# Where weights and moving operands begin in SBUF: offsets modulo 512 bytes

## The chip, the cores and the metric

The kernel runs on one core of a Trainium2 chip as one launch. The metric is the device time of that launch in microseconds. Three runs of the kernel before took 1084.68, 1085.39 and 1087.12 us (median 1085.39); the profiled execution, from which all rows come, took 1085.86 us, of which 1084.1 us are the span from its first to its last instruction.

## The reference

A sequence of 256 tokens of width 1024 goes through three blocks, all in float32. Each block is a mixer followed by a squared-ReLU MLP of width 4096; the three mixers differ. The dense products carry most of the arithmetic:

```python
for l in range(DEPTH):                       # block 1
    h = _rmsnorm(x, ln_mix_g[l])
    proj = h @ w_in[l]                       # 1024 x 7748: attention, HGRN, convolution, gates
    ...
    mixed = (g[:, :, 0] * (y_attn @ w_up_attn[l]) + g[:, :, 1] * (y_hgrn @ w_up_hgrn[l])
             + g[:, :, 2] * (y_conv @ w_up_conv[l]))
    x = x + mixed @ w_out[l]
    h = _rmsnorm(x, ln_mlp_g[l])
    x = x + jnp.square(jax.nn.relu(h @ w_mlp_up[l])) @ w_mlp_down[l]
...
def even_mixer(h, w_in, b_forget, rel_bias, w_out):            # block 2
    qa, ka, va, fa, qb, kb, vb = _split(h @ w_in, SPLIT_AB)
    ...
    return o @ w_out
def odd_mixer(h, positions, w_in, q_norm, kv_norm, w_uq, w_ukv, w_out):   # block 3
    qc, kc, vc, c_q, c_kv, k_r = _split(h @ w_in, SPLIT_CD)
    ...
    return o @ w_out
def squared_relu_mlp(h, w_up, w_down):                         # blocks 2 and 3
    return jnp.square(jax.nn.relu(h @ w_up)) @ w_down
```

## The kernel before

Activations lie transposed: 128 partitions by 8 blocks of 256 tokens. All weights of the program are one stream of 128x128 blocks in the order of their use. SyncE loads the stream in pieces of 2048 columns into `stg` (three buffers). `take` (L163) splits each 1024 columns, 8 blocks, into two parts that TensorE multiplies in one pass each: ScalarE writes the high part `whi` (L173), VectorE the rest `wlo` (L175), five buffers each. Activations are split in the same way: `operand` (L304) writes the high part `xh` and the rest `xl` of the normalized input of a mixer or an MLP, `oh`, `ol` hold the heads' outputs of mixers 2 and 3, `mh`, `ml` the mixed branches of mixer 1, and `hid` the MLP's hidden layer, high part and rest side by side in 512 columns.

A product of one weight block and one activation block is three matmuls of 256 columns (`gemm`, L230, L233, L234): whi with the high part, whi with the rest, wlo with the high part. Each has its own load of 128x128 weights ahead of it. `gemm_wide` (L242, L243) makes the same three products in two matmuls, since `hid` holds both parts side by side: whi with 512 columns, then wlo with the first 256. It is used for seven of the eight output blocks of each down projection; the eighth uses `gemm`. `gemm_tokens` (L269) exchanges the sides: slices of `xh` and `xl` are the loaded weights, and 256 columns of whi or wlo stream.

The order of the work around is set by the program's text and by a scheduler that works from a model of the engines' times: `slot` hands pieces of attention to the engines between output blocks of the dense products, and each engine then has one fixed queue. Weight pieces, ScalarE's and VectorE's splits and attention's softmax run beside TensorE.

Where tiles lie: the pools are laid out one behind another. Small tiles in the pool `keep` (`eps`, `half`, `rtok`, of 4 or 8 bytes, 32 bytes of room each) stand ahead of the weights' pools, so that stg, whi and wlo begin 32 bytes past a multiple of 512. A weight block is 512 bytes in a partition and a block of 256 activations is 1024, so that within a stage every moving operand begins at one and the same distance, modulo 512, from the weights. In the kernel before this distance (moving operand less weights) is 416 bytes for xh and xl in all six stages, 288 for mh and ml, and 0 for hid, oh, ol, the branches' operands and the latents of mixer 3.

In mixer 3 a rotated key is made in the tile `kr` (L1069 to L1076) and two rotated queries in `zr` (two buffers, L1081 to L1086); each is done with `rope` on VectorE and GpSimd.

Of the kernel before, what the change touches and what calls it, by code (L numbers as in the profile page):

```python
# [10 lines left out]
FP32 = mybir.dt.float32  # L11
FP32R = mybir.dt.float32r
# [6 lines left out]
T = 256  # L19
D = 1024  # L20
FF = 4096
KD = 8
# [16 lines left out]
FIRST = 256  # L39

RA, RB, RC = 1.0, 1.5, 1.5

GROUPS_MIX = [range(0, 8)]
GROUPS_ATT = [range(0, 4), range(4, 6), range(6, 8)]
# [20 lines left out]
def _mid(ap, n):  # L65

    return ap.unsqueeze(1).to_broadcast([ap.shape[0], n, ap.shape[1]])
# [8 lines left out]
def kernel(  # L76
# [18 lines left out]
    def pool(name, bufs=1, space=None, stack=ctx):  # L95
        kw = {"space": space} if space is not None else {}
        return stack.enter_context(tc.tile_pool(name=name, bufs=bufs, **kw))

    keep = pool("keep")
# [10 lines left out]
    xv = keep.tile([128, NVEC + KD * T], FP32, name="xv")  # L110
    vec = xv[:, 0:NVEC]
    x = xv[:, NVEC:].rearrange("p (k t) -> p k t", k=KD)
    xh = keep.tile([128, KD, T], FP32R, name="xh")
    xl = keep.tile([128, KD, T], FP32R, name="xl")
    cst = keep.tile([128, NCONST], FP32, name="cst")
    ones = keep.tile([128, 128], FP32, name="ones")
    sqa = keep.tile([128, T], FP32, name="sqa")
    staged = {}

# [12 lines left out]
    load(1)  # L132
    nc.sync.dma_start(out=cst, in_=consts)
    nc.vector.memset(ones, 1.0)
    eps = keep.tile([128, 1], FP32, name="eps")
    nc.vector.memset(eps, EPS)

    half = keep.tile([128, 2], FP32, name="half")
    nc.gpsimd.memset(half, 0.0)
    for g in range(2):  # L140
        nc.gpsimd.memset(half[64 * g:64 * g + 64, g:g + 1], HD ** -0.5)
# [6 lines left out]
    def v_(name, j=0):  # L148
        o = VOFF[name][0] + j
        return vec[:, o:o + 1]  # L150
# [60 lines left out]
    def slot(steps=1):  # L211
        for d in list(due):
            d[0] -= 1
            if d[0] <= 0:
                due.remove(d)
                d[1]()
        credit[0] = credit[0] + steps if chains else 0
        while credit[0] >= 1:
            credit[0] -= 1
            step()  # L220

    def drain():
        while due or chains:
            slot()
# [22 lines left out]
    def gemm1(kt, ah, al, steps=1):  # L247
        ks = kt if isinstance(kt, range) else range(kt)
        ps = pg_p.tile([128, 2, T], FP32, name="pg")
        gemm(ps[:, 0], ks, ah, al)  # L250
        slot(steps * len(ks) / KD)
        return ps[:, 0]
# [51 lines left out]
    def operand(j, gain):  # L304

        nc.scalar.activation(out=xh[:, j], in_=x[:, j], func=AF.Copy, scale=v_(gain, j))
        nc.vector.scalar_tensor_tensor(out=xl[:, j], in0=x[:, j], scalar=v_(gain, j), in1=xh[:, j],  # L307
                                       op0=ALU.mult, op1=ALU.subtract)
# [16 lines left out]
    def sum_squares():  # L325
        ps = po_p.tile([128, 2, T], FP32, name="po")
        nc.tensor.matmul(out=ps[:, 0], lhsT=ones, rhs=sqa, start=True, stop=False)
        nc.tensor.matmul(out=ps[:, 0], lhsT=ones, rhs=sq_last["s"], start=False, stop=True)
        return ps[:, 0]
# [1 line left out]
    rstd = keep.tile([128, T], FP32, name="rstd")  # L331
    rvar = keep.tile([128, T], FP32, name="rvar")

    rtok = keep.tile([128, 2], FP32, name="rtok")

    def rstd_tokens():

# [8 lines left out]
    def residual(ah, al, groups, gain):  # L346


        for ks in groups[:-1]:
            for j in range(KD):  # L350
                nc.vector.tensor_tensor(out=x[:, j], in0=gemm1(ks, ah, al, RC), in1=x[:, j], op=ALU.add)
        drain()
        for j in range(KD):
            nc.vector.tensor_tensor(out=x[:, j], in0=gemm1(groups[-1], ah, al), in1=x[:, j], op=ALU.add)
            operand(j, gain)
            squares(j)

    def mlp(gain_next):
        def variance():
            u = tmp.tile([128, 512], FP32, name="rs_u", bufs=1)[:, 0:T]  # L360
            nc.vector.tensor_scalar(out=u, in0=sum_squares(), scalar1=1.0 / D, scalar2=EPS, op0=ALU.mult, op1=ALU.add)
            nc.vector.reciprocal(out=rvar, in_=u)

        variance()
        with ExitStack() as st:
            hp = pool("hid", stack=st)
            mp = pool("mlpt", 2, stack=st)
            hid = hp.tile([128, FF // 128, 2, T], FP32R, name="hid")
            for j in range(0, FF // 128, 2):
                ps = gemm2(KD, xh, xl)  # L370
                r = mp.tile([128, 2, T], FP32, name="r")
                s = mp.tile([128, 2, T], FP32, name="s")
                nc.scalar.activation(out=r, in_=ps, func=AF.Relu)
                nc.scalar.activation(out=hid[:, j:j + 2, 0], in_=r, func=AF.Square)
                nc.vector.scalar_tensor_tensor(out=s, in0=ps, scalar=0.0, in1=r, op0=ALU.max, op1=ALU.mult)
                nc.vector.tensor_tensor(out=hid[:, j:j + 2, 1], in0=s, in1=hid[:, j:j + 2, 0], op=ALU.subtract)  # L376
            for j in range(KD):

                wide = j < KD - WN
                if wide:  # L380
                    ps = gemm_wide(FF // 128, hid)
                else:
                    ps = gemm1(FF // 128, hid[:, :, 0], hid[:, :, 1])

                for z in HALVES if gain_next is None and j == KD - 1 else [slice(0, T)]:
                    t = tmp.tile([128, T], FP32, name="dn")[:, z]
                    if wide:
                        nc.scalar.activation(out=t, in_=ps[:, 1], func=AF.Copy)
                        nc.vector.tensor_tensor(out=t, in0=ps[:, 0], in1=t, op=ALU.add)
                    nc.vector.tensor_tensor(out=t, in0=t if wide else ps[:, z], in1=rvar[:, z], op=ALU.mult)  # L390
                    nc.vector.tensor_tensor(out=x[:, j, z], in0=t, in1=x[:, j, z], op=ALU.add)  # L391
                    if z.stop - z.start < T:
                        nc.scalar.activation(out=rstd[:, z], in_=x[:, j, z], func=AF.Square)
                if gain_next is not None:
                    operand(j, gain_next)
                    squares(j)
                else:
                    if j < KD - 1:
                        squares(j)
                    nc.scalar.activation(out=xg[:, j], in_=x[:, j], func=AF.Copy, scale=v_("norm_final", j))  # L400
# [132 lines left out]
    with ExitStack() as st:  # L533
# [9 lines left out]
        att = pool("att1", stack=inner)  # L543
# [250 lines left out]
        for j in range(4):  # L794
# [4 lines left out]
            t = hg.tile([128, T], FP32, name="ut", bufs=2)  # L799
# [8 lines left out]
            t = hg.tile([128, T], FP32, name="ut", bufs=2)  # L808
# [9 lines left out]
        for b, (yh, yl) in enumerate(((yc_h, yc_l), (ya_h, ya_l), (yh_h, yh_l))):  # L818
            if b == 2:
                while "linear" not in events:  # L820
                    slot()
                mhp = pool("mixh", stack=late)
                mh = mhp.tile([128, KD, T], FP32R, name="mh")
                ml = mhp.tile([128, KD, T], FP32R, name="ml")
            gates = {}

            def gate(j):
                ps = gemm2(KD, xh, xl)
                z = mp.tile([128, 2, T], FP32, name="gz", bufs=1)
                gates[j] = g = mp.tile([128, 2, T], FP32, name="gg", bufs=2)  # L830
                nc.vector.tensor_tensor(out=z, in0=ps, in1=_mid(rstd, 2), op=ALU.mult)
                sigmoid(g, z, g)

            gate(0)
            for j in range(0, KD, 2):
                if j + 2 < KD:
                    gate(j + 2)
                ps = gemm2(4, yh, yl)
                mj, g = mixed[:, j:j + 2], gates.pop(j)
                if b == 0:  # L840
                    nc.vector.tensor_tensor(out=mj, in0=ps, in1=g, op=ALU.mult)
                else:
                    nc.vector.tensor_tensor(out=g, in0=ps, in1=g, op=ALU.mult)
                    (nc.vector if b == 2 else nc.gpsimd).tensor_tensor(out=mj, in0=mj, in1=g, op=ALU.add)
                if b == 2:
                    split(mh[:, j:j + 2], ml[:, j:j + 2], mj)
# [35 lines left out]
    with ExitStack() as st:  # L882
        att = pool("att2", stack=st)
        pb["p"] = 4
        oh = att.tile([128, KD, T], FP32R, name="oh")
        ol = att.tile([128, KD, T], FP32R, name="ol")
        cb = att.tile([128, 8, T], FP32, name="cb")
        nc.sync.dma_start(out=cb, in_=chk_bias)

# [85 lines left out]
    first(rsqrt(sum_squares(), T, 1.0 / D, rstd))  # L975
    with ExitStack() as st:
        att = pool("att3", stack=st)
        oh = att.tile([128, KD, T], FP32R, name="oh")
        ol = att.tile([128, KD, T], FP32R, name="ol")

        swap = [(i + ROPE_HALF) % 32 for i in range(32)]

# [85 lines left out]
        values(0)  # L1068
        cqh, cql = latent(3, "q_norm", "cq")  # L1069
        ckh, ckl = latent(2, "kv_norm", "ck")  # L1070
        kr = att.tile([128, T], FP32, name="kr")
        ps = gemm1(KD, xh, xl)
        scaled(kr[0:32], ps[0:32])
        a, b = rope(kr, 32)
# [4 lines left out]
        for j in range(2):  # L1079
            ps = gemm1(3, cqh, cql, RA)  # L1080
            zr = att.tile([128, T], FP32, name="zr", bufs=2)  # L1081
# [242 lines left out]
```

## Time and profile before

| | |
|---|---|
| median of three runs | 1085.39 us |
| profiled execution | 1085.86 us |
| its span | 1084.1 us |
| TensorE matmul busy | 1061.3 us, 98%, 8136 matmuls |
| TensorE weight load busy | 1022.7 us, 94% |
| VectorE busy | 838.4 us, 77% |
| ScalarE busy | 601.7 us, 56% |
| GpSimd busy | 156.2 us, 14% |
| HBM read | 181.57 MB, 168 GB/s over the span |

A matmul's busy time overlaps that of the next, so the 98% say that TensorE nearly always has one in flight and not how fast it goes. How fast is read from the timeline: the time from one matmul's start to the next one's, here called a step.

### The profile page before, as it was taken

Reading aid. Unit: us, or ns where it says so; the run is one execution under the profiler, and the core shown is the slowest. Engines: PE = TensorE matmul, PEld = TensorE weight load, DVE = VectorE, ACT = ScalarE, POOL = GpSimd, SP = SyncE. Lnnn points to the kernel's source line nnn. Section 1 sums busy time; section 2 is a strip of 40 time slices with the busy share of each in tenths; the row PEclk is TensorE's granted clock in tenths of the full one; section 3 lists DMA queues with packets and bytes.
Section 4 is the critical chain, followed back from the end, with each engine's and each line's share of the span. In section 5 each row is a group of like instructions: output and inputs, shape, how many; then the busy total and the mean of one; then the engine's idle time right before and its main releaser. Section 6 shows DMA issues by size and latency. Waiting matters only on the chain.

```text
span 1084.1 us, 20315 instructions
## 1 busy us (share of the span) xinstructions
PE 1061.3 (98%) x8136; PEld 1022.7 (94%) x8136; DVE 838.4 (77%) x1613; ACT 601.7 (56%) x944; POOL 156.2 (14%) x174
## 2 busy tenths in 40 slices
PE   7999999999999999999999999999999999999996
PEld 6999989999999988999999999988999999999886
DVE  7999898977996666678778867667689788666673
ACT  6467456665575544456654555444458755554441
POOL 1045550110400001120003000011121021000110
PEclk9999999999999999999999999999999999999999
DMA  8544433555455545554434555555444235555541
GB/s 299 218 161 141 154 121 117 167 189 195 156 195 195 188 182 185 185 210 146 150 130 143 179 177 190 194 194 174 173 161 164 107 118 185 170 190 194 191 159 39
DMA packets 29008, 183.94 MB, mean 170 GB/s; under 512 B 3057, under 2 KB 6385, under 8 KB 7281
## 3 DMA queue, kind: packets, MB, share of 16 engines
q1 hardware_dynamic: 28768, 182.50, 47.7%
q8 instruction: 64, 1.05, 0.4%
q14 instruction: 32, 0.25, 0.1%
q10 hardware_dynamic: 144, 0.13, 0.0%
HBM read 181.57 MB, written 1.05 MB: 168 GB/s over the span
## 4 chain that ended last, share of the span: by engine, by line
PE 90%; DVE 6%; issue 1%; ACT 1%; DMA 1%; POOL 0%; SPq 0%; DVEq 0%; POOLq 0%
PE pg L233 19%; PE pg L234 19%; PE pg L230 19%; PE pg L242 14%; PE pg L243 7%; PE pg L269 4%; DVE wlo L175 3%; PE sc L435 2%; PE po L472 2%; PE pt L465 1%; PE sc L428 1%; PE po L473 1%; DVE xl L307 1%; DMA stg<-w 1%; ACT whi L173 1%
## 5 line engine op out<-in xcount | busy, mean ns | idle before, releaser
L175 DVE TENSOR_TENSOR wlo<-stg,whi 128x512 fp32r<-128x512 f32 (+1 forms) x676 | 472.7, 740 | 163.9 <-ACT whi L173 160.8
L173 ACT ACTIVATE whi<-stg 128x1024 fp32r<-128x1024 f32 (+1 forms) x340 | 356.3, 1051 | 337.0 <-PE pg L233 191.8
L230 PE MATMUL pg<-xh,whi 128*128 128x256 f32 x1472 | 417.6, 284 | 7.3 <-ACT whi L173 6.9
L233 PE MATMUL pg<-xl,whi 128*128 128x256 f32 x1472 | 416.8, 284 | 0.9 <-DVE xl L307 0.7
L234 PE MATMUL pg<-xh,wlo 128*128 128x256 f32 x1472 | 417.1, 284 | 0.3
L230 PEld LDWEIGHTS pg<-xh,whi 128*128 128x128 f32 x1472 | 278.9, 190 | 8.6 <-ACT whi L173 7.2
L233 PEld LDWEIGHTS pg<-xl,whi 128*128 128x128 f32 x1472 | 279.0, 190 | 2.7 <-DVE xl L307 2.0
L234 PEld LDWEIGHTS pg<-xh,wlo 128*128 128x128 f32 x1472 | 278.9, 190 | 1.6 <-DVE wlo L175 1.0
L242 PE MATMUL pg<-hid,whi 128*128 128x512 f32 x672 | 233.1, 391 | 0.0
L243 PE MATMUL pg<-hid,wlo 128*128 128x256 f32 x672 | 188.2, 280 | 0.0
L242 PEld LDWEIGHTS pg<-hid,whi 128*128 128x128 f32 x672 | 125.7, 187 | 27.4
L243 PEld LDWEIGHTS pg<-hid,wlo 128*128 128x128 f32 x672 | 127.0, 189 | 0.0
L315 POOL TENSOR_TENSOR sqa<-xv 128x256 f32<-128x256 f32 x6 | 4.1, 678 | 471.4 <-DVE xv L391 304.4
L319 POOL TENSOR_TENSOR sq<-xv 128x256 f32<-128x256 f32 x36 | 26.5, 742 | 175.2 <-DVE xv L391 169.6
L455 ACT ACTIVATE p<-p,m 128x128 f32<-128x128 f32 x64 | 28.6, 448 | 17.6 <-DVE m L453 17.3
L320 POOL TENSOR_TENSOR sqa<-sqa,sq 128x256 f32<-128x256 f32 x36 | 36.9, 1024 | 2.3
L233 PE MATMUL pg<-ol,whi 128*128 128x256 f32 x128 | 36.8, 289 | 0.1
L269 PE MATMUL pg<-whi,xl 128*128 128x256 f32 x128 | 36.6, 286 | 0.0
L269 PE MATMUL pg<-whi,xh 128*128 128x256 f32 x128 | 36.4, 284 | 0.0
L234 PE MATMUL pg<-oh,wlo 128*128 128x256 f32 x128 | 36.3, 286 | 0.0
L269 PE MATMUL pg<-wlo,xh 128*128 128x256 f32 x128 | 36.2, 283 | 0.0
L376 DVE TENSOR_TENSOR hid<-s,hid 128x512 fp32r<-128x512 f32 x48 | 33.1, 690 | 4.0
(361 smaller groups left out, 1589.8 us busy)
## 6 DMA issues: line engine op xcount, KB each, us to landing
stg<-w SPq DMA_DIRECT2D x168, 1024.0 KB, 4.8
t<-t_bias SPq DMA_DIRECT2D x8, 128.0 KB, 2.9
cb<-chk_bias SPq DMA_DIRECT2D x1, 1024.0 KB, 4.8
xv<-x_in SPq DMA_DIRECT2D x2, 384.0 KB, 6.3
cst<-consts SPq DMA_DIRECT2D x1, 640.0 KB, 11.2
stg<-w SPq DMA_DIRECT2D x1, 512.0 KB, 8.1
out<-xg SPq DMA_DIRECT2D x2, 256.0 KB, 2.9
stg<-w SPq DMA_DIRECT2D x1, 384.0 KB, 6.8
```

Source lines behind the costliest of these rows:

```text
L173: act = [nc.scalar.activation(out=h[:, z], in_=src[:, z], func=AF.Copy) for z in (pieces if u == 0 else [slice(0, UW)])]
L175: dve = [nc.vector.tensor_tensor(out=l[:, z], in0=src[:, z], in1=h[:, z], op=ALU.subtract) for z in pieces]
L230: m0 = nc.tensor.matmul(out=ps, lhsT=h, rhs=ah[:, k], start=(k == ks[0]), stop=False)
L233: nc.tensor.matmul(out=ps, lhsT=h, rhs=al[:, k], start=False, stop=False)
L234: m1 = nc.tensor.matmul(out=ps, lhsT=l, rhs=ah[:, k], start=False, stop=(k == ks[-1]))
L242: nc.tensor.matmul(out=ps, lhsT=h, rhs=a[:, k], start=(k == 0), stop=False)
L243: nc.tensor.matmul(out=ps[:, 1], lhsT=l, rhs=a[:, k, 0], start=False, stop=(k == kt - 1))
L269: nc.tensor.matmul(out=ps, lhsT=a[:, k, t], rhs=w_, start=(k == 0 and i == 0), stop=(k == kt - 1 and i == 2))
L319: nc.gpsimd.tensor_tensor(out=s, in0=x[:, j], in1=x[:, j], op=ALU.mult)
L320: nc.gpsimd.tensor_tensor(out=sqa, in0=sqa, in1=s, op=ALU.add)
L376: nc.vector.tensor_tensor(out=hid[:, j:j + 2, 1], in0=s, in1=hid[:, j:j + 2, 0], op=ALU.subtract)
L455: nc.scalar.activation(out=p[:, a:b], in_=p[:, a:b], func=AF.Exp, scale=-1.0, bias=m[:, i:i + 1], accum_out=sums[:, i:i + 1])
```

## The change

Small tiles of `keep` are put into one tile `few`, so that stg, whi and wlo begin at a multiple of 512 bytes. The tiles of moving operands get 512 bytes more (`ROOM`), and the operand is put at an offset within: `xh` and `xl` are views of one tile `xo`, placed anew for each of the six stages that `PLACES` names, `hid` by `HIDDEN`, mh and ml by `MIXED`, oh and ol by `HEADS` (all in elements of 4 bytes). To make room, `kr` becomes one of the two `zr` buffers.

Distance of the moving operand from the weights modulo 512 bytes:

| stage | operand | before | after |
|---|---|---|---|
| mixer 1 | xh, xl | 416 | 64 |
| mixer 1, output | mh, ml | 288 | 352 |
| MLP 1, up | xh, xl | 416 | 192 |
| MLP 1, down | hid | 0 | 64 |
| mixer 2 | xh, xl | 416 | 32 |
| mixer 2, output | oh, ol | 0 | 64 |
| MLP 2, up | xh, xl | 416 | 320 |
| MLP 2, down | hid | 0 | 192 |
| mixer 3 | xh, xl | 416 | 16 |
| mixer 3, output | oh, ol | 0 | 448 |
| MLP 3, up | xh, xl | 416 | 448 |
| MLP 3, down | hid | 0 | 32 |
| mixer 1, branches; mixer 3, latents | ya, yh, yc; cq, ck | 0 | 0 |

```diff
+ROOM = 128
+PLACES = {"block1": 32, "ln_mlp_g": 64, "norm_mix0": 24, "norm_mlp0": 96, "norm_mix1": 20, "norm_mlp1": 0}
+HIDDEN = {"norm_mix0": 16, "norm_mix1": 48, None: 8}
+MIXED = 16
+HEADS = [16, 112]
...
-    xh = keep.tile([128, KD, T], FP32R, name="xh")
-    xl = keep.tile([128, KD, T], FP32R, name="xl")
+    xo = keep.tile([128, 2 * KD * T + ROOM], FP32R, name="xo")
+
+    def placed(t, n, at):
+        return t[:, at:at + n * T].rearrange("p (k t) -> p k t", k=n)
+
+    def place(stage):
+        nonlocal xh, xl
+        at = PLACES[stage]
+        xh, xl = placed(xo, KD, at), placed(xo, KD, at + KD * T)
...
+    few = keep.tile([128, 16], FP32, name="few")
...
-    eps = keep.tile([128, 1], FP32, name="eps")
+    eps = few[:, 0:1]
...
-    half = keep.tile([128, 2], FP32, name="half")
+    half = few[:, 1:3]
...
-    rtok = keep.tile([128, 2], FP32, name="rtok")
+    rtok = few[:, 4:6]
...
         drain()
+        place(gain)
         for j in range(KD):
...
-            hid = hp.tile([128, FF // 128, 2, T], FP32R, name="hid")
+            hid = hp.tile([128, FF // 128 * 2 * T + ROOM], FP32R, name="hid")
+            hid = placed(hid, FF // 128 * 2, HIDDEN[gain_next]).rearrange("p (k i) t -> p k i t", i=2)
...
+            if gain_next is not None:
+                place(gain_next)
...
-        oh = att.tile([128, KD, T], FP32R, name="oh")
-        ol = att.tile([128, KD, T], FP32R, name="ol")
+        oh = placed(att.tile([128, KD * T + ROOM], FP32R, name="oh"), KD, HEADS[0])
+        ol = placed(att.tile([128, KD * T + ROOM], FP32R, name="ol"), KD, HEADS[0])
...
-        kr = att.tile([128, T], FP32, name="kr")
+        kr = att.tile([128, T], FP32, name="zr", bufs=2)
```

No instruction is added to the engines' work or taken from it. In mixers 1 and 2, in the MLPs and on SyncE and GpSimd the queues hold the same instructions in the same order; in mixer 3 the scheduler puts 10 instructions of ScalarE, 13 of VectorE and 105 of TensorE at other places, two of which follow.

ScalarE in mixer 3, from the second `zr` copy on: `s` is a softplus of the stick-breaking heads, `ck_h` the high part of a latent, `qm` queries, `pT` transposed probabilities. Before:

```order
544 L1082 ACTIVATE zr<-pg 128x256 x2
545 L173 ACTIVATE whi<-stg 128x1024
546 L1090 ACTIVATE qm<-pg 64x256 x2
547 L467 ACTIVATE pT<-pt 128x384
548 L1090 ACTIVATE qm<-pg 64x256 x2
549 L293 ACTIVATE s<-sc 128x384
550 L278 ACTIVATE ck_h<-ck_raw 128x512
551 L294 ACTIVATE s<-s 128x384
552 L1090 ACTIVATE qm<-pg 64x256 x2
```

The same place of ScalarE's queue now:

```order
544 L1106 ACTIVATE zr<-pg 128x256 x2
545 L193 ACTIVATE whi<-stg 128x1024
546 L1114 ACTIVATE qm<-pg 64x256 x2
547 L491 ACTIVATE pT<-pt 128x384
548 L1114 ACTIVATE qm<-pg 64x256 x2
549 L313 ACTIVATE s<-sc 128x384
550 L314 ACTIVATE s<-s 128x384
551 L298 ACTIVATE ck_h<-ck_raw 128x512
552 L1114 ACTIVATE qm<-pg 64x256 x2
```

The split of `ck_h` now stands behind the second step of the softplus. The second `zr` copy has a new wait: its buffer was `kr`, which VectorE must have copied into `km` (L1076, now L1100).

TensorE in mixer 3, ahead of the second product that has tokens on its output rows: the scores of a latent head (`sc<-km,qm`). Before:

```order
6042 L230 MATMUL pg<-xh,whi 128x256
6043 L233 MATMUL pg<-xl,whi 128x256
6044 L428 MATMUL sc<-km,qm 128x128
6045 L435 MATMUL sc<-km,qm 128x256
6046 L234 MATMUL pg<-xh,wlo 128x256
6047 L269 MATMUL pg<-whi,xh 128x256
6048 L269 MATMUL pg<-whi,xl 128x256
```

The same place of TensorE's queue now:

```order
5935 L254 MATMUL pg<-xo,wlo 128x256
5936 L452 MATMUL sc<-km,qm 128x128
5937 L459 MATMUL sc<-km,qm 128x256
5938 L250 MATMUL pg<-xo,whi 128x256
5939 L253 MATMUL pg<-xo,whi 128x256
5940 L254 MATMUL pg<-xo,wlo 128x256
5941 L289 MATMUL pg<-whi,xo 128x256 x2
```

The scores stand two matmuls of 256 columns earlier against the dense product.

## Rows read from the trace of the kernel before

**Rows 1.** The page's head, its busy times, and the chain that ended last.

```profile
span 1084.1 us, 20315 instructions
...
PE 1061.3 (98%) x8136; PEld 1022.7 (94%) x8136; DVE 838.4 (77%) x1613; ACT 601.7 (56%) x944; POOL 156.2 (14%) x174
...
PE 90%; DVE 6%; issue 1%; ACT 1%; DMA 1%; POOL 0%; SPq 0%; DVEq 0%; POOLq 0%
```

**Rows 2.** The costliest groups of TensorE: shapes, count, then busy us, mean ns.

```profile
L230 PE MATMUL pg<-xh,whi 128*128 128x256 f32 x1472 | 417.6, 284 | 7.3 <-ACT whi L173 6.9
...
L242 PE MATMUL pg<-hid,whi 128*128 128x512 f32 x672 | 233.1, 391 | 0.0
L243 PE MATMUL pg<-hid,wlo 128*128 128x256 f32 x672 | 188.2, 280 | 0.0
...
L269 PE MATMUL pg<-whi,xl 128*128 128x256 f32 x128 | 36.6, 286 | 0.0
...
L234 PE MATMUL pg<-oh,wlo 128*128 128x256 f32 x128 | 36.3, 286 | 0.0
```

**Rows 3.** Timeline, TensorE, up projection of MLP 1: start us, duration us, instruction.

```profile
319.96 0.28 PE L234 MATMUL pg<-xh,wlo 128*128 128x256 f32 x1
...
337.56 0.28 PE L234 MATMUL pg<-xh,wlo 128*128 128x256 f32 x1
```

**Rows 4.** Timeline, TensorE, up projection of MLP 2.

```profile
619.94 0.28 PE L233 MATMUL pg<-xl,whi 128*128 128x256 f32 x1
...
637.74 0.28 PE L233 MATMUL pg<-xl,whi 128*128 128x256 f32 x1
```

**Rows 5.** Timeline, TensorE, up projection of MLP 3.

```profile
919.92 0.28 PE L234 MATMUL pg<-xh,wlo 128*128 128x256 f32 x1
...
937.92 0.28 PE L234 MATMUL pg<-xh,wlo 128*128 128x256 f32 x1
```

**Rows 6.** Timeline, TensorE, output projection of mixer 2.

```profile
581.63 0.28 PE L230 MATMUL pg<-oh,whi 128*128 128x256 f32 x1
...
587.63 0.28 PE L234 MATMUL pg<-oh,wlo 128*128 128x256 f32 x1
```

**Rows 7.** Timeline, TensorE, wide down projection of MLP 1.

```profile
400.01 0.39 PE L242 MATMUL pg<-hid,whi 128*128 128x512 f32 x1
...
406.95 0.39 PE L242 MATMUL pg<-hid,whi 128*128 128x512 f32 x1
```

**Rows 8.** Timeline, TensorE, a product with tokens on the rows, mixer 1.

```profile
67.79 0.28 PE L269 MATMUL pg<-whi,xl 128*128 128x256 f32 x1
...
70.19 0.28 PE L269 MATMUL pg<-whi,xh 128*128 128x256 f32 x1
```

**Rows 9.** Timeline, TensorE, mixer 3: three transposes merged into one row.

```profile
818.78 0.49 PE L465 MATMUL pt<-cst,p 128*128 128x128 f32 x3
```

**Rows 10.** Line 465, the transposes: durations ns min/median/max, first and last start.

```profile
L465 PE MATMUL pt<-cst,p x120: 270/272/275, 89.1 to 881.2; 128*128 128x128 f32 x120
```

**Rows 11.** Busy us and count by stretch, mixer 1: PE, PEld, DVE, ACT, POOL.

```profile
20.00:60.00 40.00, 40.00 (x329) 39.64 (x328) 39.26 (x111) 22.11 (x29) 2.81 (x3) 1.00 0.56 202
60.00:100.00 40.00, 40.00 (x333) 39.73 (x332) 39.49 (x89) 25.13 (x52) 20.06 (x16) 1.00 0.48 169
...
150.00:200.00 50.00, 47.37 (x384) 46.08 (x383) 43.16 (x68) 30.59 (x46) 7.25 (x3) 1.00 0.38 130
```

**Rows 12.** Timeline, VectorE, mixer 3: the copy of kr into km.

```profile
812.33 1.22 DVE L1076 COPY km<-kr 32x2048 f32<-32x2048 f32 x1
```

**Rows 13.** Timeline, ScalarE, mixer 3: second zr copy, and the two exchanged instructions.

```profile
813.69 0.38 ACT L1082 ACTIVATE zr<-pg 128x256 f32<-128x256 f32 x1 [0.70 <-PE pg L234]
...
817.91 0.63 ACT L278 ACTIVATE ck_h<-ck_raw 128x512 fp32r<-128x512 f32 x1 [0.22 <-DVE ck_raw L1008]
818.45 0.51 ACT L294 ACTIVATE s<-s 128x384 f32<-128x384 f32 x1
```

More of the change, by code (lines that the diff above doesn't have):

```diff
@@ L112 @@
     x = xv[:, NVEC:].rearrange("p (k t) -> p k t", k=KD)
-    xh = keep.tile([128, KD, T], FP32R, name="xh")
-    xl = keep.tile([128, KD, T], FP32R, name="xl")
+    xo = keep.tile([128, 2 * KD * T + ROOM], FP32R, name="xo")
[5 more added lines that the diff above has]
+        xh, xl = placed(xo, KD, at), placed(xo, KD, at + KD * T)
+    xh = xl = None
+    place("block1")
     cst = keep.tile([128, NCONST], FP32, name="cst")
     ones = keep.tile([128, 128], FP32, name="ones")
+    few = keep.tile([128, 16], FP32, name="few")
     sqa = keep.tile([128, T], FP32, name="sqa")
@@ L822 @@
                 mhp = pool("mixh", stack=late)
-                mh = mhp.tile([128, KD, T], FP32R, name="mh")
-                ml = mhp.tile([128, KD, T], FP32R, name="ml")
+                mh = placed(mhp.tile([128, KD * T + ROOM], FP32R, name="mh"), KD, MIXED)
+                ml = placed(mhp.tile([128, KD * T + ROOM], FP32R, name="ml"), KD, MIXED)
             gates = {}
@@ L977 @@
         att = pool("att3", stack=st)
-        oh = att.tile([128, KD, T], FP32R, name="oh")
-        ol = att.tile([128, KD, T], FP32R, name="ol")
+        oh = placed(att.tile([128, KD * T + ROOM], FP32R, name="oh"), KD, HEADS[1])
+        ol = placed(att.tile([128, KD * T + ROOM], FP32R, name="ol"), KD, HEADS[1])
         swap = [(i + ROPE_HALF) % 32 for i in range(32)]
```

## The prediction

> **What bounds the kernel now.** I read the page first. TensorE has a matmul in flight for 1061.3 of 1084.1 us and carries 90% of the chain that ended last; VectorE is busy for 77%, ScalarE for 56% [rows 1]. So the time is set by how fast matmuls follow each other. The groups by line do not tell this: they give a mean of 284 ns for a matmul of 256 columns [rows 2], but neighbours overlap. The timeline does, from start to start. I took 150 matmuls in the same place of each of the three up projections, which run the same code on tiles at the same addresses, with no wait in between. The first needs 337.56 - 319.96 = 17.60 us for 150 steps, 117.3 ns each [rows 3]; the second 17.80 us, 118.7 ns [rows 4]; the third 18.00 us, 120.0 ns [rows 5]. The granted clock is 1.00, 2.4 GHz [rows 11], at which 256 columns are 106.7 ns. So each matmul pays 10.7 to 13.3 ns over its columns, a tenth of the time, and what it pays differs between stages that differ in nothing but the way they were entered. The three paces stand at equal distances of 1.33 ns.
>
> Where the moving operand has distance 0 from the weights, I found one pace only: 50 steps of the output projection of mixer 2 take 6.00 us, 120.0 ns [rows 6]. The wide down projection takes 6.94 us for 20 pairs, 347 ns a pair [rows 7], for 768 columns that are 320 ns at full clock: 27 ns over, 13.5 per weight load, as much as at 120. The products with tokens on the rows, whose loaded side is xh and xl, take 2.40 us for 20 steps, 120.0 [rows 8].
>
> What else could make a step longer than 106.7? The weight load beside it: one of 128 columns goes with every matmul. The transposes bound its share. Three of them fill 0.49 us and the last one takes 0.272 [rows 9, 10], so two steps take 0.22 us, 109 ns each, with a full weight load in each. A load alone thus allows 109 ns. What is left, 8 to 11 ns, appears where 256 columns stream at full rate while the next weights load. Both are reads of SBUF, and both addresses are what this change moves.
>
> **The change part by part.** It adds no matmul, no DMA and no byte of traffic. It changes the distances, orders mixer 3 a little differently and adds one wait.
>
> The distance. No row shows any of the new distances, so the pace there is bounded from both sides. Below: 109 ns, what a load needs by itself. Above: one more step of 1.33 ns over the slowest pace, 121.3. Distance 416 gave three paces and distance 0 the slowest of the three always; so the distance counts, and 0 is a bad one. For the new ones I take one step of 1.33 ns under the fastest pace seen, 116.0, the value next to [rows 3]; 109 has no matmul of this kind behind it. Then:
>
> - The three up projections have 32 x 8 x 3 = 768 steps each. They win 1.3, 2.7 and 4.0 ns a step: 768 x 8.0 = 6.1 us.
> - xh and xl are used in 3 x 1472 = 4416 steps [rows 2] (one of three alike). The 2112 outside the up projections I put at 118.7, the middle pace: 2112 x 2.7 = 5.7 us.
> - oh and ol, 3 x 128 steps [rows 2] (one of three alike), and the eighth output block of each down projection, 3 x 96, leave distance 0: 672 x 4 = 2.7 us.
> - The products with tokens, 3 x 128 steps [rows 2] (one of three alike), go from 120 to 116: 1.5 us.
> - The wide pairs, 672 [rows 2], hold two weight loads each. If each is relieved as above, a pair falls by 8 ns: 5.4 us.
> - mh and ml, 192 steps, move from 288 to 352. I give them nothing.
>
> That is 21.4 us. Not all of it reaches the end. Between 20 and 100 us VectorE, which makes wlo, is busy for 39.3 and 39.5 of 40 us [rows 11]; the 540 or so steps there that win 2.7 ns, and some 100 of products with tokens, run into VectorE instead: 1.9 us less. From 150 to 200 us TensorE is idle for 2.6 us waiting for others [rows 11], and the other mixers have such places too; a faster TensorE waits there longer. For this I take off another 1.5 us. Left: 18 us.
>
> Mixer 3. The second zr copy waits for the copy of kr, which ended at 812.33 + 1.22 = 813.55 us; the zr copy began at 813.69 [rows 12, 13], so the wait has 0.14 us to spare. If it came late, the weight split whi behind it on ScalarE would be late by as much. The exchange of ck_h with a softplus step delays ck_h by 0.51 us [rows 13], and its reader on VectorE after it; TensorE has transposes, scores and values of two heads to do at that moment [rows 9], the first of them. I put both at 0, at most 0.5 us together, and the scores that stand two matmuls earlier at 0, at most 0.24 us either way.
>
> The tile `few`, the merged `xo` and the beginnings of stg: no instruction gets another size, the splits of weights and activations stay off the path in the MLPs, where VectorE and ScalarE have room. Zero.
>
> The sum is made against the profiled execution: 1085.9 - 18.0 = 1067.9 us. That execution was 0.5 us over the median, so I say 1067.5.
>
> The Trainium skill speaks against all this. In "TensorE: Matmul & The Clock Gate", section "Step-by-step: what each phase is for", it says that TensorE has two independent read ports of SBUF, one for the streaming operand and one for weight loads, so that a load takes no bandwidth from the running matmul. By that rule no distance can matter and the time stays at 1085.4. The same page gives, under "Back-to-back issue gap", columns over clock plus 2.5 ns, 109 ns for 256 columns, as the gap of an isolated matmul; by the trace 117 to 120 are paid, so here something more than these two ports is at work.
>
> **The rivals.**
>
> Slower. The pace is a pattern that locks, as three paces from one layout show; a new distance may lock at a worse one. Place: the up projections and the wide pairs, where nothing interrupts the pattern for 90 us. Price: 121.3 ns instead of 118.4 on average for 4416 steps is 12.8 us, 1.3 ns for 1056 steps from 120 is 1.4, two loads in 672 pairs 1.8: 16 us, 1101 us. It decides as soon as the mean step on xh and xl is over 118.4. Against it: the distance 0 that is left is the slowest seen.
>
> No change by distance. The pace depends only on the phase in which a stage is entered, and the change merely shuffles 117.3, 118.7 and 120.0 among the stages. For it: rows 3 to 5 have one distance and three paces. Price: all up projections at 117.3 win 768 x 4.0 = 3.1 us, all at 120.0 lose as much: 1082 to 1089, in the middle no change.
>
> More. The new distances avoid the collisions nearly altogether, and the steps come half way to 109, at 113. Then xh and xl win 4416 x 5.4 = 23.8 us, the 1056 steps from distance 0 win 7 ns, 7.4 us, the pairs 14 ns, 9.4 us; 40.6, less some 6 in front of VectorE and in the mixers: 1051 us. For it: a weight load does allow 109. Against it: nothing of the kind was seen in four operands.
>
> **How the numbers follow.** The forecast, 1056 to 1079, has 0.55; more, 0.14; no change by distance, 0.18; slower, 0.13. A difference under 0.2%, 2.2 us, cannot be told from none here. Of the rival without effect of distance, 0.08 falls on faster, 0.08 on within 0.2%, 0.02 on slower, and of slower 0.01 within. That makes faster 0.77, same 0.09, slower 0.14. The range that leaves out 2 in 10 goes from 1050, the rival with more, to 1086, no change.
>
> **What would show it.** Right: 150 steps of each up projection take 17.4 us or less; the output projections of mixers 2 and 3 leave 120.0; a wide pair takes 339 ns; the branches ya, yh, yc and the latents, still at distance 0, stay at 120; VectorE's busy share between 20 and 100 us stays near full while the span of that stretch hardly shrinks. Wrong: a pair stays at 347 while the narrow steps fall (then 5.4 us are missing); new distances show the old three paces; or one stage locks at 121 or more. If the steps fall and the span does not, the waits of TensorE in the mixers have grown by as much.

## The result, and the profile after

The changed kernel takes 1079.76 us (median of 4 runs, 1076.93 to 1080.11), the kernel before 1085.3. The ratio is 0.9942, 95% interval 0.9929 to 0.9954: 5.5 us less, where 18 were forecast. The profiled execution took 1079.46 us.

The page of the changed kernel, its span, busy times (engine, us, share, count) and TensorE's two groups of the down projection (line, shapes, count, then busy us, mean ns):

```profile
span 1077.7 us, 20317 instructions
...
PE 1055.1 (98%) x8136; PEld 1015.3 (94%) x8136; DVE 836.2 (78%) x1613; ACT 602.0 (56%) x944; POOL 158.8 (15%) x174
...
L262 PE MATMUL pg<-hid,whi 128*128 128x512 f32 x672 | 235.1, 394 | 0.0
L263 PE MATMUL pg<-hid,wlo 128*128 128x256 f32 x672 | 188.9, 281 | 0.0
```

TensorE has 6.2 us less in flight than in [rows 1], nearly the 6.4 that the span lost. But the wide pairs, which were to win most for each step, have grown against [rows 2]: from 233.1 to 235.1 and from 188.2 to 188.9 us.

Where the time went shows when the timeline is cut at the first matmul of each stage (us, worked out from these starts; each a difference of two of them):

| stage | before | after | 416/0 again | hid 32 | all 112 | 112 and branches |
|---|---|---|---|---|---|---|
| mixer 1 with output | 286.1 | 283.6 | 285.2 | 284.8 | 283.0 | 278.9 |
| MLP 1 up | 92.8 | 92.1 | 94.0 | 92.1 | 89.8 | 89.8 |
| MLP 1 down | 89.2 | 89.5 | 89.2 | 88.9 | 88.9 | 88.9 |
| mixer 2 with output | 121.9 | 120.5 | 121.9 | 120.5 | 120.0 | 120.0 |
| MLP 2 up | 93.3 | 92.9 | 92.4 | 92.9 | 89.7 | 89.7 |
| MLP 2 down | 89.2 | 90.5 | 90.7 | 88.9 | 88.9 | 88.9 |
| mixer 3 with output | 118.0 | 117.3 | 118.1 | 117.3 | 116.8 | 116.8 |
| MLP 3 up | 94.1 | 92.6 | 92.4 | 89.7 | 89.6 | 89.6 |
| MLP 3 down | 89.2 | 88.9 | 90.7 | 88.9 | 88.9 | 88.9 |

(The last four columns are experiments, below.) From the unrounded starts the mixers won 4.5 us, the up projections 2.7, the end 0.5; the down projections lost 1.3.

The row of mixer 1 has to be read with care. It opens with TensorE waiting for the first weights (most of the 6.9 us behind whi in [rows 2]) and then with steps of 213 ns, and this opening is not equally long in every run. The first 20 us before, after, with all 112, and with 112 and branches (stretch, its length, then busy us and count of TensorE, its weight loads, VectorE, ScalarE and GpSimd, clock, share of the DMA engines, GB/s):

```profile
0.00:20.00 20.00, 12.92 (x70) 11.81 (x71) 14.29 (x34) 12.59 (x24) 3.72 (x15) 1.00 0.90 328
...
0.00:20.00 20.00, 13.26 (x83) 12.13 (x84) 15.50 (x38) 13.85 (x25) 3.71 (x15) 1.00 0.89 332
...
0.00:20.00 20.00, 12.13 (x64) 11.02 (x65) 13.61 (x33) 11.79 (x23) 3.71 (x15) 1.00 0.90 320
...
0.00:20.00 20.00, 13.08 (x82) 11.97 (x83) 15.35 (x38) 13.65 (x25) 3.71 (x15) 1.00 0.90 329
```

TensorE gets through 70, 83, 64 and 82 matmuls of one and the same queue: the steps of 213 ns give way to some 118 at 15.0, 11.9, 15.8 and 12.5 us, while the clock reads 1.00 in all four. The 81st matmul starts at 21.2, 19.7, 21.9 and 19.9 us; with hid at 32, where mixer 1 is that of the changed kernel, at 21.1. So 1.5 of the mixers' 4.5 us are a shorter opening, which the distances don't explain; from the 81st matmul on the mixers won 3.0.

The timeline of TensorE after (start us, duration us, instruction): 150 steps in each up projection, in the places of [rows 3 to 5].

```profile
320.00 0.28 PE L253 MATMUL pg<-xo,whi 128*128 128x256 f32 x1
...
337.67 0.28 PE L253 MATMUL pg<-xo,whi 128*128 128x256 f32 x1
...
640.03 0.28 PE L250 MATMUL pg<-xo,whi 128*128 128x256 f32 x1
...
657.70 0.28 PE L250 MATMUL pg<-xo,whi 128*128 128x256 f32 x1
...
940.12 0.28 PE L253 MATMUL pg<-xo,whi 128*128 128x256 f32 x1
...
957.78 0.28 PE L253 MATMUL pg<-xo,whi 128*128 128x256 f32 x1
```

17.67 us each, 117.8 ns a step, at three different distances (192, 320, 448). Before it was one distance and three paces, now, in the profiled execution, it is three distances and one pace. Yet the third stage had begun faster. The same timeline at its beginning:

```profile
892.71 0.28 PE L254 MATMUL pg<-xo,wlo 128*128 128x256 f32 x1
...
894.75 0.28 PE L254 MATMUL pg<-xo,wlo 128*128 128x256 f32 x1
...
896.62 0.59 PE L347 MATMUL po<-sqa,ones 128*128 128x256 f32 x2
897.05 0.59 PE L348 MATMUL po<-sq,ones 128*128 128x256 f32 x2
```

The first two lines are 18 steps apart, 113.3 ns each, at the same distance 448. Then the two full-precision matmuls that sum the squares pass, and behind them it is 117.8 to the end of the stage. The down projections, 20 wide pairs in MLP 1, 2 and 3 (distance 64, 192, 32):

```profile
400.02 0.28 PE L263 MATMUL pg<-hid,wlo 128*128 128x256 f32 x1
...
407.00 0.28 PE L263 MATMUL pg<-hid,wlo 128*128 128x256 f32 x1
...
700.09 0.40 PE L262 MATMUL pg<-hid,whi 128*128 128x512 f32 x1
...
707.16 0.40 PE L262 MATMUL pg<-hid,whi 128*128 128x512 f32 x1
...
1000.03 0.39 PE L262 MATMUL pg<-hid,whi 128*128 128x512 f32 x1
...
1006.96 0.39 PE L262 MATMUL pg<-hid,whi 128*128 128x512 f32 x1
```

349, 353 and 347 ns a pair: none is under the 347 of distance 0 in [rows 7]. The output projections of mixer 2 (distance 64, to be held against [rows 6]) and mixer 1 (352):

```profile
577.07 0.28 PE L250 MATMUL pg<-oh,whi 128*128 128x256 f32 x1
...
582.74 0.28 PE L254 MATMUL pg<-oh,wlo 128*128 128x256 f32 x1
...
267.07 0.28 PE L250 MATMUL pg<-mh,whi 128*128 128x256 f32 x1
...
273.06 0.28 PE L254 MATMUL pg<-mh,wlo 128*128 128x256 f32 x1
```

50 steps each: 5.67 us, 113.4 ns, in mixer 2; 5.99 us, 119.8 ns, in mixer 1. The new wait in mixer 3, for [rows 12, 13], on ScalarE and VectorE:

```profile
808.86 0.38 ACT L1106 ACTIVATE zr<-pg 128x256 f32<-128x256 f32 x1
810.10 0.38 ACT L1106 ACTIVATE zr<-pg 128x256 f32<-128x256 f32 x1 [0.85 <-DVE km L1100]
...
808.79 1.22 DVE L1100 COPY km<-zr 32x2048 f32<-32x2048 f32 x1
```

The second copy now waits for the copy into km, and comes 1.24 us behind the first instead of 1.08. Mixer 3 is shorter all the same.

### The profile page after: what moved, and what is told of

Read it like the earlier page. It is cut to its first block, busy times and chain, and to the rows that moved or that the text cites. A ratio compares the mean times of both kernels' runs of the same rounds, so it can differ in the third digit from the quotient of the medians.

```text
span 1077.7 us, 20317 instructions
## 1 busy us (share of the span) xinstructions
PE 1055.1 (98%) x8136; PEld 1015.3 (94%) x8136; DVE 836.2 (78%) x1613; ACT 602.0 (56%) x944; POOL 158.8 (15%) x174
## 5 line engine op out<-in xcount | busy, mean ns | idle before, releaser
L250 PE MATMUL pg<-xo,whi 128*128 128x256 f32 x1472 | 415.7, 283 | 7.5 <-ACT whi L193 6.5
L254 PE MATMUL pg<-xo,wlo 128*128 128x256 f32 x1472 | 415.0, 282 | 0.4 <-DVE wlo L195 0.3
L253 PE MATMUL pg<-xo,whi 128*128 128x256 f32 x1472 | 414.4, 282 | 0.6 <-DVE xo L327 0.6
L250 PEld LDWEIGHTS pg<-xo,whi 128*128 128x128 f32 x1472 | 276.6, 188 | 8.9 <-ACT whi L193 6.8
L254 PEld LDWEIGHTS pg<-xo,wlo 128*128 128x128 f32 x1472 | 278.8, 190 | 1.7 <-DVE wlo L195 1.1
L253 PEld LDWEIGHTS pg<-xo,whi 128*128 128x128 f32 x1472 | 276.9, 188 | 2.1 <-DVE xo L327 1.3
L262 PE MATMUL pg<-hid,whi 128*128 128x512 f32 x672 | 235.1, 394 | 0.0
L263 PE MATMUL pg<-hid,wlo 128*128 128x256 f32 x672 | 188.9, 281 | 0.0
L289 PE MATMUL pg<-whi,xo 128*128 128x256 f32 x256 | 47.5, 283 | 0.0
L289 PEld LDWEIGHTS pg<-whi,xo 128*128 128x128 f32 x256 | 39.5, 188 | 0.1
L289 PE MATMUL pg<-wlo,xo 128*128 128x256 f32 x128 | 36.0, 281 | 0.0
```

The costliest lines, as they stand in the source:

```text
L250: m0 = nc.tensor.matmul(out=ps, lhsT=h, rhs=ah[:, k], start=(k == ks[0]), stop=False)
L253: nc.tensor.matmul(out=ps, lhsT=h, rhs=al[:, k], start=False, stop=False)
L254: m1 = nc.tensor.matmul(out=ps, lhsT=l, rhs=ah[:, k], start=False, stop=(k == ks[-1]))
L262: nc.tensor.matmul(out=ps, lhsT=h, rhs=a[:, k], start=(k == 0), stop=False)
L263: nc.tensor.matmul(out=ps[:, 1], lhsT=l, rhs=a[:, k, 0], start=False, stop=(k == kt - 1))
L289: nc.tensor.matmul(out=ps, lhsT=a[:, k, t], rhs=w_, start=(k == 0 and i == 0), stop=(k == kt - 1 and i == 2))
```

## The experiments

Theories: A, the distance alone sets the pace; B, it is where the weights begin; C, the distance allows a short list of paces, and what stands ahead of a chain picks from it.

**The old distances in the new layout.** `PLACES` all 120, `MIXED` and `HEADS` 0, `HIDDEN` 0:

```diff
-HIDDEN = {"norm_mix0": 16, "norm_mix1": 48, None: 8}
-MIXED = 16
+HIDDEN = {"norm_mix0": 0, "norm_mix1": 0, None: 0}
+MIXED = 0
```

> This is the changed kernel with one thing undone: weights still begin at multiples of 512 bytes and the tiles are the new, larger ones, but every moving operand gets the distance it had before (416, 0, 288). Theory A (the gain comes from the distances): the paces of before return, 117.3 to 120.0 ns in the up projections, 347 ns a wide pair in all three MLPs, and the time goes back to 1085 us, +5 us on the changed kernel, ratio to before 1.000 +- 0.002. Theory B (the gain comes from where the weights begin, or from the order in mixer 3): it keeps the time of the changed kernel, 1080 us, ratio 0.995. Theory C (only the phase of entry counts): between the two, with the paces of the three MLPs shuffled.

1085.16 us, ratio to before 0.9996 (0.9987 to 1.0004). The whole gain is gone, so it comes from the distances; the new beginnings of the weights and the order of mixer 3 are worth nothing that can be measured. (Stage by stage it is not the same: against the kernel before, the up projections are 1.4 us shorter here and the down projections 3.0 longer.) The up projections of MLP 1 and 2 on its timeline:

```profile
320.09 0.28 PE L254 MATMUL pg<-xo,wlo 128*128 128x256 f32 x1
...
338.09 0.28 PE L254 MATMUL pg<-xo,wlo 128*128 128x256 f32 x1
...
640.10 0.28 PE L250 MATMUL pg<-xo,whi 128*128 128x256 f32 x1
...
657.70 0.28 PE L250 MATMUL pg<-xo,whi 128*128 128x256 f32 x1
```

120.0 and 117.3 ns (MLP 3: 117.3), where [rows 3 to 5] have 117.3, 118.7, 120.0: the list of paces is the same, the stages have drawn others from it. The wide pairs, too, at distance 0: 346.7 ns in MLP 1, 353.2 in MLP 2 and 3, where all three had 346.7 before. So A alone doesn't hold.

**The new distances on shifted weights.**

```diff
-        at = PLACES[stage]
+        at = PLACES[stage] + 8
-    few = keep.tile([128, 16], FP32, name="few")
+    few = keep.tile([128, 24], FP32, name="few")
```

> The changed kernel with weights beginning 32 bytes past a multiple of 512, as they did before, and all moving operands shifted by the same 32 bytes, so that every distance is the one of the changed kernel and only the common origin moves. Theory A (only the distance counts): the same paces as in the changed kernel, up projections 117.8 ns, wide pairs 349, 353 and 347 ns, time 1080 us within 1.5 us. Theory B (weights want to begin at multiples of 512 bytes): paces move back towards 117.3 to 120.0 and the time to 1085 us.

1080.88 us, ratio 0.9948 (0.9928 to 0.9967), as the changed kernel. Up projections 117.8, wide pairs of MLP 2 353.3 and of MLP 3 346.7 ns. With this one other origin the gain stays, which is against theory B. But the pairs of MLP 1 took 353.2 ns where theory A expected 349: distance 64, too, has two paces.

**A scan of distances.** A kernel of chains alone, 48 narrow steps (256 columns) or 16 wide pairs (512 and 256), each after a wait and again behind two full-precision matmuls:

```python
for d in range(0, 512, 16):
    wait()
    narrow(d, 96, full, [48])
    wait()
    wide(d, 32, full, [16])
```

> Leaves out the whole computation: it holds only chains of matmuls like those of the kernel, 256 moving columns (narrow) and pairs of 512 and 256 columns (wide), with the moving operand at each distance 0, 16, ..., 496 from the weights; for each distance 48 narrow steps after a wait, two full-precision matmuls, 48 more narrow steps, a wait, 16 wide pairs, the same two matmuls, 16 more pairs. Theory A (distance sets the pace): one pace per distance, the same ahead of the two matmuls and behind them, 120 ns at distance 0, 117 to 120 at 416 and 113 to 118 at 64, 192, 320, 448; a wide pair 347 at 0, 349 at 64, 353 at 192. Theory C (distance only sets which paces are possible, the entry picks one): at the same distance the 48 steps ahead and behind differ at several distances, for example 113.3 on one side and 117.8 on the other at 64 or 192. Theory P (independent reads, no effect of address): one pace near 109 ns everywhere.

Distances that are equal modulo 256 show paces from the same list. At most distances the two chains agree, at 16, 64, 144, 160 and a few others they differ (64: 117.8 and 113.3). Wide pairs take 346.7 ns at 16, 32, 144, 160 and 256 bytes above these, 346.7 or 353.3 at 0, and 349 to 354 elsewhere. No narrow chain was under 113.3, no pair under 346.6.

**What picks from the list.** Chains of 36 steps at distances 64, 192, 320 and 32, parted by one matmul of 16 to 256 columns:

```python
cols = [16 * c for c in range(1, 17)]
narrow(d, 36 * 34, lambda i: part((cols * 2)[i] if i < 32 else 256), ...)
```

> Leaves out the whole computation: chains of 36 narrow steps at distances 64, 192, 320 and 32, parted by one extra matmul of 16, 32, ..., 256 columns, each length twice. Theory C (the phase of entry picks the pace): at one distance both 113.3 and 117.8 ns are seen, which of them goes with the length of the extra matmul, and the second pass over the lengths gives the same list as the first or one that depends on the pace before it. Theory A (the distance alone): one pace at each distance, whatever the extra matmul.

At 192, 11 of 34 chains ran at 113.3, the others at 117.8, no other pace. At 64 and 320 all 33 behind an extra matmul were at 117.8. At 32, 21 at 116.7, 12 at 117.8. Two neighbours at 192 on the timeline, each chain in one row (start, duration, count):

```profile
164.97 0.17 PE L48 MATMUL po<-M,W 128*128 128x16 f32 x1
164.99 4.49 PE L48 MATMUL pg<-M,W 128*128 128x256 f32 x36
...
173.67 0.18 PE L48 MATMUL po<-M,W 128*128 128x48 f32 x1
173.69 4.34 PE L48 MATMUL pg<-M,W 128*128 128x256 f32 x36
```

35 steps differ by 0.15 us, 4.3 ns each, with all addresses alike. That is theory C. The length of the extra matmul alone does not decide: behind 48 columns the first pass gave 113.3, the second 117.8.

**hid at 32 in all three MLPs.**

```diff
-HIDDEN = {"norm_mix0": 16, "norm_mix1": 48, None: 8}
+HIDDEN = {"norm_mix0": 8, "norm_mix1": 8, None: 8}
```

> The changed kernel with the moving operand of the down projection at distance 32 in all three MLPs (it was 64, 192, 32), all else the same. Theory C (a distance allows a short list of paces): the wide pair takes 346.7 ns in all three MLPs, as in the scan at 32 and as in MLP 3 of the changed kernel, so MLP 1 wins 224 x 2.2 ns = 0.5 us and MLP 2 224 x 6.7 ns = 1.5 us: 2.0 us less than the changed kernel, 1078 us. Theory D (the wide pair depends on how the stage is entered, not on the distance): still 349 and 353, 1080 us.

1075.40 us, ratio 0.9902 (0.9889 to 0.9915): 4.4 us under the changed kernel instead of 2.0. Its timeline, a stretch of 150 steps in the up projection of MLP 3 and 20 pairs in MLP 2:

```profile
940.05 0.28 PE L253 MATMUL pg<-xo,whi 128*128 128x256 f32 x1
...
957.05 0.28 PE L253 MATMUL pg<-xo,whi 128*128 128x256 f32 x1
...
700.15 0.28 PE L263 MATMUL pg<-hid,wlo 128*128 128x256 f32 x1
...
707.09 0.28 PE L263 MATMUL pg<-hid,wlo 128*128 128x256 f32 x1
```

The pairs came to 346.7 ns as expected (down projections 0.6 + 1.6 us, by the table). The rest was not foreseen: MLP 3, whose distance did not change, now runs at 113.3, 2.9 us less. That is theory C in the kernel itself. The last 11 steps ahead of the two matmuls that sum the squares:

```profile
894.35 0.28 PE L254 MATMUL pg<-xo,wlo 128*128 128x256 f32 x1
...
895.65 0.28 PE L253 MATMUL pg<-xo,whi 128*128 128x256 f32 x1
```

Some 118 ns each; behind the two it is 113.3. In the changed kernel it was the other way round.

**All of xh, xl, mh, ml, oh, ol at 112 or 368.** `PLACES` all 44, `HIDDEN` all 8:

```diff
-MIXED = 16
-HEADS = [16, 112]
+MIXED = 20
+HEADS = [28, 28]
```

> The changed kernel with xh, xl, oh, ol, mh and ml at distance 112 or 368 (the same modulo 256) in every stage, where the scan showed 113.3 ns in four of four chains, and hid at 32. Theory C (112 allows 113.3 alone, so the entry no longer matters): up projections at 113.3 ns in all three MLPs, that is 3 x 768 x 4.4 ns = 10.2 us, the other 2112 steps on xh and xl some 3 to 4 ns less, 7 us, wide pairs 2.0 us, less some 4 us that VectorE and the waits of the mixers take back: 1064 us, between 1060 and 1070. Theory E (four chains were luck, the kernel's own entries bring other paces): up projections at 117 to 118 in one or more MLPs and 1072 to 1078 us.

1066.01 us, ratio 0.9814 (0.9802 to 0.9827). All three up projections hold 113.3 ns; that of MLP 2:

```profile
640.11 0.28 PE L250 MATMUL pg<-xo,whi 128*128 128x256 f32 x1
...
657.11 0.28 PE L250 MATMUL pg<-xo,whi 128*128 128x256 f32 x1
```

They win 8.4 us against the changed kernel, the down projections 2.2, the mixers only 1.6. Here the opening took 2.2 us more; from the 81st matmul on the mixers win 3.8. In the mixers the products with tokens, where xo is the loaded side and the sign of the distance turns, went from 113.3 or 118.3 to 120.0 ns, and between 20 and 100 us VectorE is busy for 39.4 and 39.7 of 40 us.

**192 or 448 in place of 112.** `PLACES` all 64, `MIXED` 40, `HEADS` 48 and 48.

> The same kernel with distance 192 or 448 in place of 112. Theory C: 192 allows 113.3 and 117.8, and what stands ahead picks one (14 of 34 chains were at 113.3 in the bench, all four in the scan), so the stages differ among themselves: some stretches at 113.3, the up projections behind the variance matmuls at 117.8 as in the changed kernel; 1066 to 1077 us, slower than the kernel at 112. Theory A (distance alone): 192 gives one pace in all stages.

1074.39 us, ratio 0.9884 (0.9864 to 0.9903), one run at 1068.48. Some stretches at 113.3 (mixer 1's output, 100 steps in 11.33 us), all three up projections at 117.8. The expectation counted 14 chains of 34 at 113.3 in the bench, it was 11. The kernel at 112 is 8.4 us faster by the medians: a distance with one fast pace beats one whose list merely contains it.

**A finer scan.** The same bench in steps of 8 bytes, seven entries for narrow, four for wide:

```python
for d in range(0, 256, 8):
    wait()
    narrow(d, 28 * 7, lambda i: part(cols[i]), [28 * i + 28 for i in range(6)])
```

> Leaves out the whole computation: chains of narrow steps at distances 0, 8, ..., 248 and of wide pairs at 0, 8, ..., 120, each distance entered once after a wait and then behind an extra matmul of 16 to 240 columns (six entries more for narrow, three for wide). Theory C: a distance shows one pace or a list of two or three, never a pace outside its list, all seven narrow chains at 112 take 113.3 ns, those at 192 either 113.3 or 117.8, at 0 they take 120; wide pairs take 346.7 at 16 to 32 and 350 to 353 at 48 to 112. Theory E: 112 shows 117 or more behind some of the extra matmuls.

Paces seen in the three benches (ns, start to start within a chain once it repeats):

| distance mod 256 | narrow | | distance | wide pair |
|---|---|---|---|---|
| 0 | 120.0 in 11 of 11 | | 0 | 346.7, 353.3 |
| 16 | 113.3, 116.7, 118.7 | | 16 | 346.7 only |
| 32 | 116.7, 117.8 | | 32 | 346.7 only |
| 64 | 113.3, 117.8 | | 48 | 346.7, 350, 351 |
| 96 | 120.0 | | 64 | 348.9, 353.3 |
| 104, 120 | 120 to 122 | | 80 | 350.0, 353.3 |
| 112 | 113.3 in 11 of 11 | | 96 | 350.0 |
| 160 | 117.3, 118.7, 120.0 | | 112 | 353.3 |
| 192 | 113.3, 117.8 | | 24, 72, 120 | 352 to 360 |

The kernels' stages keep to these lists: 416 is 160, the three paces of before; 352 is 96, the 120.0 of mh after; 192, 320 and 448 are 64 and 192. The products with tokens do not always: at 112 their distance with the sign turned is 144 modulo 256, where the chains took 116.7 or 118.8, and they took 120.0. The bench moved activations only.

**The sum of squares behind the up projection.** No work added or left out:

```diff
-        variance()
         with ExitStack() as st:
...
+            variance()
             if gain_next is not None:
```

> The changed kernel with all its distances; only the two matmuls that sum the squares move, in each MLP from the beginning of the up projection to its end, ahead of the down projection. No operation is added or left out. Theory C (the distance gives the list 113.3 and 117.8, what stands ahead picks): the up projection of MLP 3, whose first 20 steps were at 113.3 until these matmuls came, now holds 113.3 for all 768 steps and wins 3.4 us; MLP 1 and 2 win 3.4 us each or nothing: 1076, 1073 or 1069.5 us. Theory F (a long stage at these distances falls to 117.8 by itself, the short stretches at 113.3 were only beginnings): all three at 117.8 and 1080 us.

1078.72 us, ratio 0.9935 (0.9920 to 0.9950); six runs fall into two groups, 1075.09 and 1075.12, and 1078.69 to 1079.01. The profiled one is of the lower. MLP 1 and MLP 2, 150 steps each:

```profile
320.04 0.28 PE L253 MATMUL pg<-xo,whi 128*128 128x256 f32 x1
...
337.04 0.28 PE L253 MATMUL pg<-xo,whi 128*128 128x256 f32 x1
...
640.03 0.28 PE L250 MATMUL pg<-xo,whi 128*128 128x256 f32 x1
...
657.69 0.28 PE L250 MATMUL pg<-xo,whi 128*128 128x256 f32 x1
```

113.3, 117.8 and (MLP 3) 113.3, for which 1073 us were expected: long stages can hold the fast pace at the very distances of the changed kernel, which is against theory F. The groups lie 3.7 us apart, about one stage's 768 x 4.4 ns = 3.4; which stage differs in the other runs no profile shows. The wide pairs of MLP 1 meanwhile drew 353.3 instead of 348.9, 1.0 us lost.

**The branches of mixer 1 at 112 too**, on top of all 112:

```diff
-        ya_h = mixp.tile([128, 4, T], FP32R, name="ya_h")
...
+        ys = mixp.tile([128, 6 * 4 * T + ROOM], FP32R, name="ys")
+        ya_h, ya_l, yh_h, yh_l, yc_h, yc_l = [placed(ys, 4, YS + 4 * T * i) for i in range(6)]
```

> The kernel with all of xh, xl, oh, ol, mh, ml at 112 or 368 and hid at 32, and in addition the six operands of the branches of mixer 1 (ya, yh, yc; 288 steps, so far at distance 0 and 120.0 ns) at 112. Theory C: these steps take 113.3, 288 x 6.7 ns = 1.9 us, so 1064 us against 1066. If other work of mixer 1 is what ends last there, it stays at 1066.

1063.52 us, ratio 0.9804 (0.9791 to 0.9817), the fastest version. Against its own runs of before it wins 21.5 us, the one without this step 19.9; the 1.7 between them agree with the expected 1.9, but the two intervals overlap. The 4.1 us between the two in the table are more than the step is worth: 2.1 are the opening, and from the 81st matmul to MLP 1 it is 259.1 against 261.1 us, 2.0 less. Its page:

```profile
span 1061.4 us, 20317 instructions
...
PE 1038.0 (98%) x8136; PEld 1000.4 (94%) x8136; DVE 836.0 (79%) x1613; ACT 601.9 (57%) x944; POOL 159.1 (15%) x174
```

**What a step pays by its columns.** Chains of 32 steps with 128 to 512 columns at four distances:

```python
for d in (0, 32, 112, 192):
    for c in (128, 192, 256, 320, 384, 448, 512):
        wait()
        sized(d, c, 96, [32, 64])
```

> Leaves out the whole computation: chains of steps with 128, 192, 256, 320, 384, 448 and 512 moving columns at distances 0, 32, 112 and 192, a new weight load of 128 columns with each. Theory H (what a step pays over its columns is a cost of each weight load, set by the distance): at 112 each size pays about 6.7 ns and at 0 about 13.3 ns, whatever its columns; 512 columns take 220 and 227 ns. Theory G (moving reads collide at a rate): the extra grows with the columns, at distance 0 from 6.7 ns with 128 to 27 with 512.

The timeline at 112, with 128, 192, 256 and 320 columns:

```profile
246.28 3.77 PE L48 MATMUL pg<-M,W 128*128 128x128 f32 x32
...
257.69 3.80 PE L48 MATMUL pg<-M,W 128*128 128x192 f32 x32
...
269.22 3.91 PE L48 MATMUL pg<-M,W 128*128 128x256 f32 x32
...
282.01 4.94 PE L48 MATMUL pg<-M,W 128*128 128x320 f32 x32
```

From start to start 111.7 ns with 128 and with 192 columns: under this no step with its own weight load came. 256 columns at 113.3 are 1.7 over it. With 320 and 384 columns a step pays 13.3 ns over its columns at all four distances (once 14.6), with 448 and 512 13.3 to 20.0. So the growth of theory G, to 27 ns with 512 columns at distance 0, is not there: it is 13.3. Theory H holds at distance 0 from 256 columns on (16.0 with 448); the 6.7 at 112 only 256 columns got.

The beginning of the bench, at distance 0, has to be left out. Its first 32 steps with 128 columns, then the first 32 with 192:

```profile
9.38 7.19 PE L48 MATMUL pg<-M,W 128*128 128x128 f32 x32 [9.38 <-ACT M L42]
...
30.98 5.92 PE L48 MATMUL pg<-M,W 128*128 128x192 f32 x32 [0.34 <-DVE W L55]
```

The steps with 128 columns take 213.3 ns to the end of their chain, and so do the first 20 or so with 192, which then go on at 111.7. The other benches, too, begin with steps of 213.3 ns, with 256 columns at distance 0 and at 64, and so do the whole kernels. They belong to the beginning of a run and not to a distance; the granted clock reads 1.00 there, too, and no row says why.

## Why the prediction failed

- **The wide pairs are the step that failed with the wrong sign.** "If each is relieved as above, a pair falls by 8 ns: 5.4 us." It rose by 2.2, 6.7 and 0 ns: 224 x 8.9 = 2.0 us lost. With the eighth blocks, 0.7 won where 1.2 were forecast, the down projections are 1.3 us longer, against 6.6 shorter in the sum: 7.9 us of the miss. With 3.4 in the up projections and 0.8 in the mixers, less 0.5 at the end, that is the whole way from 18.0 to the 6.4 us by which the span fell. I had taken the 27 ns over the columns for something that a distance must be able to relieve; the scans show no distance under 346.6, and 0, whose list is 346.7 and 353.3, had drawn the better one three times.
- **The pace of the up projections was mis-sized.** "For the new ones I take one step of 1.33 ns under the fastest pace seen, 116.0": it was 117.8. By the paces that is 768 x 2.7 = 2.0 us, by the stages 2.7, not 6.1. No single pace could be taken: their lists hold 113.3 and 117.8, and in the profiled execution all three stages drew the slow one. So the size of the gain is in part luck; one of the four runs took 1076.93 us, 2.5 under the next, and no profile shows why.
- **The mixers were mis-sized as well, and the total hides it.** The mixers with their output projections won 4.5 us; the terms of the sum for them (5.7 and 1.5 for xh and xl with the tokens, 1.5 for oh and ol, less the 3.4 hidden) make 5.3. But 1.5 of the 4.5 are the opening, which is luck, and 3.0 are left. "The 2112 outside the up projections I put at 118.7" and at 116.0: where steps follow each other without a wait they took 118.1 ns before and 116.9 after, 2112 x 1.2 = 2.5 us instead of 5.7. VectorE still works 39.6 of the 40 us from 20 on, as in [rows 11]. mh and ml, "I give them nothing", went from 117.8 to 120.0 ns: 192 x 2.2 = 0.4 us lost. The wait of the second zr came 0.16 us late, near the 0 that I put.
- **The rivals.** "No change by distance" named the right cause, entry, for what distance leaves open, and its 1082 to 1089 lies just above the result; but old distances give 1085 back and 112 gives 1066, so distance does count. "More" had the right pace, 113, and the wrong distances; its pairs, 14 ns faster, no distance gave. "Slower" was the wide pairs in part. The Trainium skill ("TensorE: Matmul & The Clock Gate", "Step-by-step: what each phase is for") names two independent read ports, one for the streaming operand and one for weight loads; by that rule alone distance would have no effect. The ratio 0.9814 at distance 112 against 0.9996 at the old ones shows that it has one.
- The error behind both: three paces at one distance meant that a distance does not have a pace but a list. I read them as noise around one number and moved that number.

## What to carry to other kernels

Where a kernel is bound by back-to-back matmuls, read the pace from start to start in long stretches, stage by stage, and ask first how far it is from the floor. If the same addresses show several paces, a layout must be judged by its list under many entries, not by one profile: choose the distance whose worst pace is good (112 here for 256 columns, 16 or 32 for the wide pairs), not the one whose best is. A bench of chains alone found that in one run; the kernel's up and down projections then did what the list said. Products with the sides exchanged were not in the bench, and at 112 they got slower.

## What the hardware showed that I had not expected

- The pace of narrow steps depends on the distance between moving operand and weights modulo 256 bytes, not 512, and 8 bytes can decide: 112 takes 113.3 ns, 104 and 120 take 120 to 122.
- Two chains with identical instructions and addresses settle at 113.3 or 117.8 ns and keep it: 768 steps, 90 us, until something else passes. So an unchanged stage can gain or lose some 3 us from an edit elsewhere: MLP 3 gained 2.9 when only hid moved.
- A step with a weight load takes 111.7 ns with 128 as with 192 columns. 109, my lower bound from the transposes, was not reached by any chain.
- Every run begins with steps of 213 ns, and not always for equally long: the 81st matmul of the same queue came between 19.7 and 21.9 us, a difference as large as some of the gains above. A stage that holds the opening has to be compared behind it.
- What makes a distance good, and what of the entry picks the pace, stays open: no run measured SBUF's or the array's side of it.
